# The merge of a hybrid block with its tokens stationary, and part of the weights' remainders by an adding transfer

## The chip, the core and the metric

The kernel runs on one NeuronCore of a Trainium2 chip, as one launch. The core has five engines with an instruction stream each: TensorE (PE, matrix products, with PEld for the loading of its stationary operand), VectorE (DVE), ScalarE (ACT), GpSimd (POOL) and SyncE (SP, which here issues all transfers). 16 DMA engines move data between HBM and the on-chip memory (SBUF); PE writes to a second memory, PSUM. The metric is the device time of one execution in microseconds (us); lower is better.

## What is computed

One layer of a block over 256 latent tokens of 2048 channels, with 256 context tokens beside them. All operands are fp32.

```python
u = rmsnorm(x, norm_g) * (1 + sc) + sh        # sc, sh, gt = split(silu(c) @ w_ada + b_ada)
a, g, z_c, xr, z_r, gc, gr = split(u @ w_in + b_in)          # 2048 columns each
v = depthwise_conv(a * sigmoid(g), conv_dw) + conv_dw_b      # width 31, along grid rows
y_conv = (silu(layernorm(v)) * silu(z_c)) @ w_conv_out
h = rglru(xr, forward) + rglru(xr, backward)                 # gates, short convolutions, scans
y_rnn = (h * silu(z_r)) @ w_rnn_out
y = sigmoid(gc) * y_conv + sigmoid(gr) * y_rnn               # the merge
x = rmsnorm(x + gt * (y @ w_o), final_g)
```

## The kernel before

**Products.** Each fp32 operand is split into a leading part of reduced precision (fp32r) and the remainder (`whi` and `wlo` for weights, `xh` and `xl` for activations). Each product takes three matmuls: leading by leading, leading by remainder, remainder by leading. Activations lie with the channels on the partitions, `xh[channel][tile][context or latents][token]`. The place of the context is later used for the recurrent branch's operand, then for the convolution branch's; the latents' place takes the merged result.

**Slots.** The weights are streamed in 152 blocks of 1 MB, each in two half blocks of 512 KB (`wall[s, h]`). `slot` runs one block: it asks for the loads of block s + 3 (`stage_load`), and then for each half issues that half's matmuls (`block_mms`), splits half of block s + 2 (`stage_split`), runs what was deferred and takes side work up to a budget (`run_side`). A block is 128 output channels: the 128x128 weights are stationary and 256 tokens move, 24 matmuls for each half. The slots follow `block_order`: 24 of xr and z_r, 32 of a and g, 16 of z_c, then the four matrices of the merge with 16 each, gr (72 to 87), w_rnn_out (88 to 103), gc (104 to 119) and w_conv_out (120 to 135), and 16 of w_o. The last matrix has another form already (`o_mms`): 128 tokens are stationary, 512 weight columns move, and four blocks make a chunk of 512 columns for two token tiles.

**The split.** `stage_split` has ACT make the leading part of a half block (L180), and one half later DVE subtracts it from the raw weights (L185). Raw weights have four buffers and so have the two parts. ACT thus waits until PE is through with the half block two slots back, and a load until ACT and DVE have read the raw buffer.

**Side work.** DVE's and ACT's work on the recurrence, the convolution (31 taps over 16 channel tiles, L660), the LayerNorm and the splits of its result lies in a queue of (cost, closure); `slot` takes as many as its budget allows. `BUD` (2.9 units of about a microsecond of DVE) holds from a and g through w_rnn_out, `BUD_LN` (2.6) in gc. The 64 sums for the residual gate gt (L820) come after it, two in a slot, with their own loads.

**Emptying the merge.** After a block of gr ACT takes sigmoid's tanh straight from PSUM with the channel's bias (L851). After w_rnn_out DVE multiplies (L855). gc is as gr (L863). After w_conv_out DVE multiplies and adds (L875, L876), and ACT and DVE split the sum into the latents' place (L877, helper L170 and L171), where w_o's products read it.

Of the kernel before, what the change touches and what calls it, by code (L numbers as in the profile page):

```python
# [8 lines left out]
F32 = mybir.dt.float32  # L9
# [52 lines left out]
def groups():  # L62
    """channel tiles by the order in which w_ada gives their scale and shift: (first, number)"""
    return [(k, 1) for k in range(NS1)] + [(k, 2) for k in range(NS1, KT - NE1, 2)] + [(k, 1) for k in range(KT - NE1, KT)]


def block_order():
    """the 128-channel output blocks after the first NEARLY ones: (matrix, block)"""
    seq = [("in", b) for b in XZ]
    for m in range(KT):  # L70
        seq += [("in", BA + m), ("in", BG + m)]
    seq += [("in", BZC + m) for m in range(KT)]
    seq += [("in", BGR + m) for m in range(KT)]
    seq += [("rnn", m) for m in range(KT)]
    seq += [("in", BGC + m) for m in range(KT)]
    seq += [("conv", m) for m in range(KT)]
    seq += [("o", m) for m in range(KT)]
    return seq
# [3 lines left out]
def block_kernel(ctx, tc, xcat, xtok, fgrow, par, wada, wgt, bgt, wearly, wall, wgate, out):  # L82
# [55 lines left out]
    # softplus(-lam) = max(-lam, 0) + log1p(exp(-|lam|)), log1p(e) = 2 atanh(e / (2 + e))  # L138
# [48 lines left out]

    def wsplit(raw, n=1024):
# [5 lines left out]
    def rsqrt(dst, tmp, src):  # L194
        # dst = (src + eps) ** -0.5, one Newton step on the table's value
# [7 lines left out]
    def ada_mms(acc, raw, rnd, n):  # L203
        # raw holds 8 // n channel tiles of 128 n columns of w_ada
# [7 lines left out]
    def ada_fin(row, part, k0, n):  # L212
        # sums of the four partial rows, channels to partitions
# [11 lines left out]
    def stat_mm(acc, x, i):  # L225
        # mean over channels: four column groups of the array take every fourth tile
# [10 lines left out]
    with ExitStack() as st:  # L237
# [28 lines left out]
        # with the tokens on the partitions, and back  # L266
# [27 lines left out]
        def products(m, ks, ws):  # L294
# [7 lines left out]
            # partial sums, in the end where the input's first tiles were  # L302
# [93 lines left out]
    # side work of VectorE and ScalarE between the blocks: (VectorE cost in us, closure)  # L396
# [5 lines left out]
    def defer(n, f):  # L402
        """f in n half slots"""
# [23 lines left out]
    def seg(t, d):  # L427
        # [segment][token] in the order of the scan: backward has the latents first
# [71 lines left out]
    def r_sum(h):  # L500
        # h of both directions; twice the reference's
# [30 lines left out]
    def r_tick(t):  # L532
        # stages of different half-units, interleaved so that no engine waits for itself
# [92 lines left out]
    vb = hbuf     # free by then  # L626
    tgc = vb      # the convolution's input is dead by then
# [82 lines left out]
    # LayerNorm over channels, swish, gate  # L710
# [37 lines left out]
    def ln_gates():  # L748
        # once the gate is there
# [9 lines left out]
    def ln_splits():  # L759
        # once the recurrent branch's operand is dead  # L760
# [263 lines left out]
```

## Time and profile before

| | |
|---|---|
| median of 3 runs (lowest, highest) | 1144.01 us (1144.0, 1147.85) |
| span of the profiled execution | 1142.0 us |
| the profiled execution's own time beside it | not listed apart; the runs lie from 1144.0 us |
| PE, DVE, ACT, POOL busy | 98%, 81%, 54%, 0% |
| HBM read, written | 230.25 MB, 2.10 MB |

"Busy" is time in which an engine works on an instruction; PE's matmuls overlap, so the spacing of their starts, and not their length, tells its pace. The span runs from the first to the last instruction; the measured time holds what lies around it too. A releaser, written after an arrow, is what ended an engine's wait. A stage's place in time is found by going back from the end of w_conv_out at 1043 us in steps of 16 blocks.

### The profile page before, as it was taken

To read this page: it belongs to the slowest core of one execution; us is meant where nothing else is said; L and a number is where in the kernel's file an instruction comes from. 1 tells how busy PE (TensorE), PEld (TensorE's weight loads), DVE (VectorE), ACT (ScalarE), POOL (GpSimd) and SP (SyncE) were. 2 spreads that over 40 slices of the span, in tenths; PEclk is the share of its full clock that TensorE was granted. 3 is DMA by queue.
4 is the path that set the end of the run, shared out by engine and by line. 5 is a ranking of instruction groups with operands and counts; after the bars stand their busy time and mean duration, and the time that the engine had idled before them with its cause. 6 is when DMAs were issued, how large, how long until landed. Compare 5 with 4: busy or idle time off the path is not lost.

```text
span 1142.0 us, 20720 instructions
## 1 busy us (share of the span) xinstructions
PE 1121.5 (98%) x8316; PEld 1010.7 (88%) x8316; DVE 924.9 (81%) x1528; ACT 615.1 (54%) x838; POOL 0.2 (0%) x4
## 2 busy tenths in 40 slices
PE   6999999999999999999999999999999999999996
PEld 3777778777798989999999999999999999999885
DVE  5555588789879888899998989999985977888885
ACT  3222279777888877644454444443335854444443
POOL 0000000000000000000000000000000000000000
PEclk9999999999999999999999999999999999999999
DMA  9998444233346555465555555555554569888772
GB/s 376 400 409 324 189 134 134 102 125 125 106 141 196 160 167 164 143 209 184 185 185 171 183 183 185 175 183 178 181 188 150 169 205 324 316 310 285 268 279 93
DMA packets 67635, 233.70 MB, mean 205 GB/s; under 512 B 7505, under 2 KB 11729, under 8 KB 67153
## 3 DMA queue, kind: packets, MB, share of 16 engines
q1 hardware_dynamic: 67538, 232.37, 59.5%
q8 instruction: 65, 1.06, 0.4%
q14 instruction: 32, 0.26, 0.1%
HBM read 230.25 MB, written 2.10 MB: 203 GB/s over the span
## 4 chain that ended last, share of the span: by engine, by line
PE 98%; DVE 1%; DMA 0%; ACT 0%; issue 0%; ACTq 0%; SPq 0%; DVEq 0%
PE acc L234 72%; PE o L912 8%; PE xr L234 6%; PE gate L472 5%; PE ada L209 2%; PE part L234 2%; PE ms L228 1%; DMA hbuf<-in_xcat_dram 0%; PE tp L216 0%; PE mps L228 0%; PE gps L833 0%; PE vps L228 0%; DVE sq L259 0%; DVE wlo L171 0%; PE tot L279 0%
## 5 line engine op out<-in xcount | busy, mean ns | idle before, releaser
L234 PE MATMUL acc<-xh,whi 128*128 128x256 f32 (+1 forms) x2176 | 566.8, 296 | 0.0
L234 PE MATMUL acc<-xl,whi 128*128 128x256 f32 (+1 forms) x2176 | 552.3, 289 | 0.0
L180 ACT ACTIVATE whi<-raw 128x1024 fp32r<-128x1024 f32 x304 | 321.1, 1058 | 351.0 <-PE acc L234 277.3
L234 PEld LDWEIGHTS acc<-xh,whi 128*128 128x128 f32 x2176 | 416.7, 192 | 17.8 <-issue 9.3
L234 PEld LDWEIGHTS acc<-xl,whi 128*128 128x128 f32 x2176 | 416.9, 192 | 12.5 <-issue 7.7
L185 DVE TENSOR_TENSOR wlo<-raw,whi 128x1024 fp32r<-128x1024 f32 x304 | 371.0, 1223 | 70.0 <-ACT whi L180 66.3
L234 PE MATMUL acc<-xh,wlo 128*128 128x256 f32 (+1 forms) x2176 | 319.0, 289 | 0.0
L234 PEld LDWEIGHTS acc<-xh,wlo 128*128 128x128 f32 x2176 | 288.2, 192 | 5.0
L660 DVE SCALAR_TENSOR_TENSOR cv<-hbuf,pt,cv 128x196 f32<-128x196 f32 (+14 forms) x480 | 185.9, 451 | 13.0 <-ACT cv L651 12.6
L461 DVE SCALAR_TENSOR_TENSOR xc<-xr,pt,xc 128x510 f32<-128x510 f32 (+2 forms) x96 | 71.0, 742 | 0.2
L472 PE MATMUL gate<-xc,gw 128*128 128x512 f32 x128 | 60.0, 592 | 0.0
L820 DVE SCALAR_TENSOR_TENSOR zc<-gtraw,csil,zc 128x512 f32<-128x512 f32 x64 | 47.9, 748 | 5.4 <-DMA gtraw<-in_wgt_dram 4.7
L234 PE MATMUL xr<-xh,whi 128*128 128x512 f32 x96 | 40.4, 421 | 0.4 <-ACT xh L170 0.4
L912 PE MATMUL o<-whi,xh 128*128 128x512 f32 x128 | 40.6, 399 | 0.0
L498 DVE TENSOR_TENSOR_SCAN tr<-a,ti 128x512 f32<-128x512 f32 x32 | 39.1, 1223 | 0.7
L333 ACT ACTIVATE row<-ada 128x128 f32<-128x128 f32 (+1 forms) x22 | 7.2, 326 | 60.2 <-PE ada L209 60.2
L912 PE MATMUL o<-whi,xl 128*128 128x512 f32 x128 | 39.5, 389 | 0.0
L912 PE MATMUL o<-wlo,xh 128*128 128x512 f32 x128 | 39.4, 389 | 0.0
L234 PE MATMUL xr<-xl,whi 128*128 128x512 f32 x96 | 37.7, 392 | 0.2 <-DVE xl L171 0.2
L472 PEld LDWEIGHTS gate<-xc,gw 128*128 128x128 f32 x128 | 22.8, 189 | 17.0 <-issue 13.9
L234 PE MATMUL xr<-xh,wlo 128*128 128x512 f32 x96 | 37.4, 390 | 0.0
L209 PE MATMUL ada<-adaraw,csil 128*32 128x128 f32 (+1 forms) x704 | 32.5, 324 | 1.1 <-DVE sh L218 0.9
(169 smaller groups left out, 838.1 us busy)
## 6 DMA issues: line engine op xcount, KB each, us to landing
raw<-in_wall_dram SPq DMA_DIRECT2D x304, 512.0 KB, 3.5
adaraw<-in_wada_dram SPq DMA_DIRECT2D x64, 512.0 KB, 8.5
gtraw<-in_wgt_dram SPq DMA_DIRECT2D x32, 512.0 KB, 3.9
raw<-in_wearly_dram SPq DMA_DIRECT2D x16, 512.0 KB, 9.9
gw<-in_wgate_dram SPq DMA_DIRECT2D x32, 128.0 KB, 3.2
hbuf<-in_xcat_dram SPq DMA_DIRECT2D x2, 1024.0 KB, 7.1
cv<-in_xtok_dram SPq DMA_DIRECT2D x4, 512.0 KB, 5.8
out_dram<-cv SPq DMA_DIRECT2D x6, 256.0 KB, 2.6
```

The lines of the kernel that those rows point to most:

```text
L180: A.activation(out=hi, in_=raw, func=AF.Copy)
L185: V.tensor_tensor(out=lo, in0=raw, in1=hi.bitcast(F32), op=SUB)
L209: PE.matmul(out=acc[g:g + 32, :w], lhsT=csil[:, k, :], rhs=raw[:, w * q:w * q + w], start=(k < 4), stop=(k >= KT - 4), tile_position=(0, g))
L228: PE.matmul(out=acc[32 * q:32 * q + 32, :], lhsT=ones[:, :32], rhs=x, start=(i < 4), stop=(i >= KT - 4), tile_position=(0, 32 * q))
L234: PE.matmul(out=acc, lhsT=w, rhs=x, start=(first and i == 0), stop=(last and i == n - 1))
L333: A.activation(out=row, in_=acc, func=AF.Copy)
L461: V.scalar_tensor_tensor(out=o, in0=i, scalar=w, in1=o, op0=MUL, op1=ADD)
L472: PE.matmul(out=acc, lhsT=u["gw"][:, c:c + 128], rhs=u["xc"], start=True, stop=True)
L498: V.tensor_tensor_scan(out=r(u["tr"]), data0=r(u["a"]), data1=r(u["ti"]), initial=0.0, op0=MUL, op1=ADD)
L660: V.scalar_tensor_tensor(out=o, in0=i, scalar=hdw[:, m * CW + j:m * CW + j + 1], in1=o, op0=MUL, op1=ADD)
L820: V.scalar_tensor_tensor(out=gt_chunk(c), in0=gt_raw[0][:, 512 * (k % 2):512 * (k % 2) + 512], scalar=csil[:, k, 0:1], in1=gt_chunk(c), op ...
L912: PE.matmul(out=acc, lhsT=y[:, k, 1, P * i:P * i + P], rhs=w[:, 512 * kk:512 * kk + 512], start=(k == 0 and w is hi and y is xh), stop=(k ...
```

## The change

**Form of the merge.** gr, w_rnn_out, gc and w_conv_out take the form that w_o had: the weights are packed in chunks (`chunked`), 128 tokens are stationary, 512 weight columns move (`chunk_mms`, which w_o now uses too), four slots make a chunk (`chunk_slot`, `chunks`). A half has 12 matmuls of 512 columns in place of 24 of 256. The tokens now lie on the partitions of gates and sums (`p2v`, `tgv`). The gates' bias varies along the row, so it is loaded for each chunk (`bias_load`, on SP's queue) and DVE adds it before ACT's tanh (`gate`).

**Transposes.** The merged sum has to get its channels back onto the partitions for w_o. `turn` transposes a channel tile on PE (two 128x128 transposes) and splits it into the latents' place. A chunk's four turns stand before the second, third and fourth slot of the next chunk and before the first of the one after; the last five stand behind the first halves of w_o.

**Remainders.** In slots 24 to 103, every fourth half block gets its remainder otherwise (`adding`, `wsplit_add`): ACT writes the negative leading part (a copy of the raw weights with scale -1), and a transfer issued by POOL adds the weights from HBM to it. **Budgets.** `BUD` is 3.5, the new `BUD_Y` 3.2 for gr and w_rnn_out, `BUD_LN` 3.0; the squares of the LayerNorm have 6 buffers in place of 8.

```diff
-BUD_XR, BUD_ZR, BUD_R, BUD, BUD_LN = 8.0, 2.7, 3.0, 2.9, 2.6
+BUD_XR, BUD_ZR, BUD_R, BUD, BUD_Y, BUD_LN = 8.0, 2.7, 3.0, 3.5, 3.2, 3.0
+GBB = 1
+AD0, AD1, ADN = 24, 104, 4
...
+    def wsplit_add(raw, src):
+        lo = whl_p.tile([P, 1024], F32R, tag="wlo", name="wlo")
+        A.activation(out=lo, in_=raw, func=AF.Copy, scale=-1.0)
+        nc.gpsimd.dma_start(out=lo, in_=src, accum_op=ADD)
+        return lo
...
+    def adding(s, h):
+        return AD0 <= s < AD1 and (2 * s + h) % ADN == ADN - 1
...
             raw = raws[s][h]
-            late.append(((s, h), raw, wsplit_hi(raw)))
+            hi = wsplit_hi(raw)
+            if adding(s, h):
+                parts[s, h] = hi, wsplit_add(raw, wall[s, h])
+            else:
+                late.append(((s, h), raw, hi))
...
+    def chunk_mms(acc, s, seg, kq, h, i):
+        hi, lo = parts[s, h]
+        for w, y in ((hi, xh), (hi, xl), (lo, xh)):
+            for kk in range(2):
+                k = 4 * kq + 2 * h + kk
+                PE.matmul(out=acc, lhsT=y[:, k, seg, P * i:P * i + P], rhs=w[:, 512 * kk:512 * kk + 512],
+                          start=(k == 0 and w is hi and y is xh), stop=(k == KT - 1 and w is lo))
+
+    def chunk_slot(s, seg, accs, kq, budget):
+        stage_load(s + 3)
+        for h in range(2):
+            for i in range(2):
+                chunk_mms(accs[i], s, seg, kq, h, i)
+            del parts[s, h]
+            stage_split(s + 2, h)
+            run_deferred()
+            run_side(budget / 2)
...
-    for m in range(KT):
-        acc = slot(s, lat, T, BUD)
-        A.activation(out=p2[:, m], in_=acc, func=AF.Tanh, scale=0.5, bias=hbin[:, BGR + m:BGR + m + 1])
-        s += 1
...
+    def bias_load(j, c):
+        t = tp2.tile([P, 512], F32, tag="gbias", name="gbias", bufs=GBB)
+        SP.dma_start(out=t, in_=bass.AP(brow.tensor, 2048 * j + 512 * c, [[0, P], [1, 512]]))
+        return t
+
+    def chunks(seg, budget, evac, before=None):
+        nonlocal s
+        for c in range(4):
+            accs = [psum(f"y{c}{i}") for i in range(2)]
+            for kq in range(4):
+                if before:
+                    before(c, kq)
+                chunk_slot(s, seg, accs, kq, budget)
+                s += 1
+            for i in range(2):
+                evac(c, i, accs[i])
+
+    def gate(v, c, i, acc, bias):
+        g = piece(v, c, i)
+        V.tensor_tensor(out=g, in0=acc, in1=bias, op=ADD)
+        A.activation(out=g, in_=g, func=AF.Tanh, scale=0.5)
...
+    def turn(m):
+        tps = psum("tps")[:, :T]
+        for i in range(2):
+            PE.transpose(tps[:, P * i:P * i + P], p2v[:, 2048 * i + P * m:2048 * i + P * m + P], pall("ident"))
+        split(xh[:, m, 1, :], xl[:, m, 1, :], tps)
...
+    def before_conv(c, kq):
         gt_steps(GTN)
+        m = 4 * c + kq
         if m % 2:
             o_load(m // 2)
...
+        if len(turns) > (0 if kq else 4):
+            turn(turns.popleft())
+
+    def evac_conv(c, i, acc):
+        g, t = piece(p2v, c, i), piece(tgv, c, i)
+        V.scalar_tensor_tensor(out=t, in0=t, scalar=1.0, in1=acc, op0=ADD, op1=MUL)
+        V.tensor_tensor(out=g, in0=g, in1=t, op=ADD)
+        if i:
+            turns.extend(range(4 * c, 4 * c + 4))
+
+    chunks(0, 0.0, evac_conv, before_conv)
...
                 gt_steps(GTO)
+                if turns:
+                    turn(turns.popleft())
```

On PE in w_conv_out before, the end of one block and the start of the next (`acc` is the block's sum in PSUM, `gps` a sum for gt):

```order
L234 MATMUL acc_11077<-xh,whi 128x256
L234 MATMUL acc_11077<-xl,whi 128x256
L234 MATMUL acc_11077<-xh,wlo 128x256 x8
L833 MATMUL gps<-zc,unit 128x512
L234 MATMUL acc_11150<-xh,whi 128x256
L234 MATMUL acc_11150<-xl,whi 128x256
```

The same engine and place now, one slot boundary in the second chunk (`y_9670` and `y_9671` are the sums of the two token tiles, `tps` a turn's target, `p_5045` the merged sum):

```order
L597 MATMUL y_9670<-wlo,xh 128x512 x2
L597 MATMUL y_9671<-whi,xh 128x512 x2
L597 MATMUL y_9671<-whi,xl 128x512 x2
L597 MATMUL y_9671<-wlo,xh 128x512 x2
L952 MATMUL tps<-pt,p_5045 128x128 x2
L597 MATMUL y_9670<-whi,xh 128x512 x2
L597 MATMUL y_9670<-whi,xl 128x512 x2
```

Matmuls are fewer and wider, and two transposes stand between two slots.

On DVE in w_conv_out before, one slot (`zc` takes the sums for gt, `hbuf` is the gate, `p_5033` the merged sum):

```order
L820 SCALAR_TENSOR_TENSOR zc<-gtraw,csil,zc 128x512 x2
L875 SCALAR_TENSOR_TENSOR hbuf<-hbuf,acc_10730 128x256
L876 TENSOR_TENSOR p_5033<-p_5033,hbuf 128x256
L171 TENSOR_TENSOR xl<-p_5033,xh 128x256
L185 TENSOR_TENSOR wlo<-raw,whi 128x1024 x2
```

And now, the end of the second chunk there and the first slot of the third:

```order
L188 TENSOR_TENSOR wlo<-raw,whi 128x1024 x2
L968 SCALAR_TENSOR_TENSOR hbuf<-hbuf,y_9670 128x512
L969 TENSOR_TENSOR p_5045<-p_5045,hbuf 128x512
L968 SCALAR_TENSOR_TENSOR hbuf<-hbuf,y_9671 128x512
L969 TENSOR_TENSOR p_5045<-p_5045,hbuf 128x512
L858 SCALAR_TENSOR_TENSOR zc<-gtraw,csil,zc 128x512 x2
L174 TENSOR_TENSOR xl<-tps,xh 128x256
L188 TENSOR_TENSOR wlo<-raw,whi 128x1024 x2
```

The multiplying and adding moved from each slot to the end of a chunk, four wide steps in a row; the split's subtraction now follows a transpose.

On ACT at the end of z_c before (`whi` is a leading part, `cv` the convolution's sum):

```order
L180 ACTIVATE whi<-raw 128x1024 x2
L790 ACTIVATE zc<-acc_7099,pt 128x256
L180 ACTIVATE whi<-raw 128x1024 x2
L651 ACTIVATE cv<-hbuf,pt 128x256 x2
L851 ACTIVATE p_5033<-acc_7169,hbin 128x256
L180 ACTIVATE whi<-raw 128x1024 x2
L851 ACTIVATE p_5033<-acc_7240,hbin 128x256
```

And now, on the same engine through the first chunk of gr:

```order
L183 ACTIVATE whi<-raw 128x1024 x2
L194 ACTIVATE wlo<-raw 128x1024
L828 ACTIVATE zc<-acc_7174,pt 128x256
L183 ACTIVATE whi<-raw 128x1024 x4
L194 ACTIVATE wlo<-raw 128x1024
L689 ACTIVATE cv<-hbuf,pt 128x256 x2
L183 ACTIVATE whi<-raw 128x1024 x4
L194 ACTIVATE wlo<-raw 128x1024
L915 ACTIVATE p_5045<-p_5045 128x512 x2
```

After four leading parts stands a negative copy into a remainder's buffer, and the tanh of a gate comes twice per chunk instead of once per slot.

## Rows read from the trace of the kernel before

**Rows 1.** The page, parts 1 and 4: busy time, and the chain's engines.

```profile
span 1142.0 us, 20720 instructions
...
PE 1121.5 (98%) x8316; PEld 1010.7 (88%) x8316; DVE 924.9 (81%) x1528; ACT 615.1 (54%) x838; POOL 0.2 (0%) x4
...
PE 98%; DVE 1%; DMA 0%; ACT 0%; issue 0%; ACTq 0%; SPq 0%; DVEq 0%
```

**Rows 2.** Windows: stages z_c, gr, w_rnn_out, gc and w_conv_out, with the header.

```profile
core 0: us, PE busy (x) PEld busy (x) DVE busy (x) ACT busy (x) POOL busy (x), PEclk, DMA share, GB/s
575.00:667.00 92.00, 92.00 (x765) 90.91 (x764) 83.42 (x157) 42.18 (x52) 0.00 (x0) 1.00 0.57 183
667.00:759.60 92.60, 92.60 (x770) 91.51 (x769) 82.03 (x155) 42.09 (x53) 0.00 (x0) 1.00 0.56 180
759.60:851.60 92.00, 92.00 (x764) 90.91 (x764) 86.31 (x167) 34.63 (x36) 0.00 (x0) 1.00 0.56 180
851.60:949.90 98.30, 98.30 (x817) 94.92 (x816) 70.43 (x116) 61.02 (x99) 0.00 (x0) 1.00 0.59 190
949.90:1043.00 93.10, 93.10 (x772) 92.62 (x771) 80.78 (x112) 41.39 (x50) 0.00 (x0) 1.00 0.89 315
```

**Rows 3.** Chain in order of time: start us, us, engine, out, line.

```profile
859.00 0.43 PE tot L717 x2
...
996.91 46.07 PE acc L234 x384
...
1077.37 43.56 PE o L912 x192
```

**Rows 4.** Groups by line and shape: count, busy us, mean ns, idle before.

```profile
L185 DVE TENSOR_TENSOR wlo<-raw,whi 128x1024 fp32r<-128x1024 f32 x304 | 371.0, 1223 | 70.0 <-ACT whi L180 66.3 <-ACT a L478 0.6
...
L180 ACT ACTIVATE whi<-raw 128x1024 fp32r<-128x1024 f32 x304 | 321.1, 1058 | 351.0 <-PE acc L234 277.3 <-DMA raw<-in_wall_dram 22.1 <-PE o L912 20.9
...
L820 DVE SCALAR_TENSOR_TENSOR zc<-gtraw,csil,zc 128x512 f32<-128x512 f32 x64 | 47.9, 748 | 5.4 <-DMA gtraw<-in_wgt_dram 4.7
...
L171 DVE TENSOR_TENSOR xl<-p,xh 128x256 fp32r<-128x256 f32 x16 | 6.8, 425 | 8.2 <-ACT xh L170 8.2
...
L897 DVE TENSOR_TENSOR cv<-cv,hbuf 128x512 f32<-128x512 f32 x8 | 5.5, 693 | 0.3
...
L896 DVE SCALAR_TENSOR_TENSOR hbuf<-o,zc 128x512 f32<-128x512 f32 x8 | 5.5, 687 | 4.8 <-PE o L912 4.8
```

**Rows 5.** Timeline of PE over one half block: start us, us, instruction.

```profile
700.36 0.28 PE L234 MATMUL acc<-xh,whi 128*128 128x256 f32 x1
...
702.28 1.12 PE L234 MATMUL acc<-xh,wlo 128*128 128x256 f32 x8
703.24 0.28 PE L234 MATMUL acc<-xh,whi 128*128 128x256 f32 x1
```

**Rows 6.** Timeline of ACT in the same half block.

```profile
702.48 1.06 ACT L180 ACTIVATE whi<-raw 128x1024 fp32r<-128x1024 f32 x1 [1.44 <-PE acc L234]
```

**Rows 7.** DMA issues: count, KB each, median us from issue to landing.

```profile
raw<-in_wall_dram SPq DMA_DIRECT2D x304, 512.0 KB, 3.5
...
raw<-in_wearly_dram SPq DMA_DIRECT2D x16, 512.0 KB, 9.9
```

**Rows 8.** Groups by line, DVE alone, 460 to 860 us.

```profile
L660 DVE SCALAR_TENSOR_TENSOR cv<-hbuf,pt,cv 128x196 f32<-128x196 f32 (+14 forms) x480 | 185.9, 451 | 13.0 <-ACT cv L651 12.6
L185 DVE TENSOR_TENSOR wlo<-raw,whi 128x1024 fp32r<-128x1024 f32 x136 | 166.5, 1225 | 20.3 <-ACT whi L180 18.3
...
L718 DVE COPY mean<-tot 128x256 f32<-128x256 f32 x1 | 0.4, 424 | 2.0 <-PE tot L717 2.0
L712 DVE COPY rstd<-mps 128x256 f32<-128x256 f32 x1 | 0.4, 418 | 0.0
```

**Rows 9.** The page, part 2: DMA share and GB/s in 40 slices.

```profile
DMA  9998444233346555465555555555554569888772
GB/s 376 400 409 324 189 134 134 102 125 125 106 141 196 160 167 164 143 209 184 185 185 171 183 183 185 175 183 178 181 188 150 169 205 324 316 310 285 268 279 93
```

More of the change, by code (lines that the diff above doesn't have):

```diff
@@ L29 @@
 TA, TB, TC, TD = 1, 2, 1, 1
+AD0, AD1, ADN = 24, 104, 4
 SG = 4
+CHUNKED = ("gr", "rnn", "gc", "conv", "o")
 BA, BG, BZC, BXR, BZR, BGC, BGR = 0, 16, 32, 48, 64, 80, 96
@@ L72, in block_order, with block_kernel @@
     seq += [("in", BZC + m) for m in range(KT)]
[L73 to L77, printed above, removed]
+    for a in CHUNKED:
+        seq += [(a, m) for m in range(KT)]
     return seq
 @with_exitstack
-def block_kernel(ctx, tc, xcat, xtok, fgrow, par, wada, wgt, bgt, wearly, wall, wgate, out):
+def block_kernel(ctx, tc, xcat, xtok, fgrow, brow, par, wada, wgt, bgt, wearly, wall, wgate, out):
     nc = tc.nc
@@ L847, in o_load @@
             SP.dma_start(out=fgb[:, c:c + 1024], in_=bass.AP(fgrow.tensor, c, [[0, P], [1, 1024]]))
-    for m in range(KT):
-        acc = slot(s, lat, T, BUD)
-        A.activation(out=p2[:, m], in_=acc, func=AF.Tanh, scale=0.5, bias=hbin[:, BGR + m:BGR + m + 1])
-        s += 1
-    for m in range(KT):
-        acc = slot(s, ctxp, T, BUD)
-        V.scalar_tensor_tensor(out=p2[:, m], in0=p2[:, m], scalar=1.0, in1=acc, op0=ADD, op1=MUL)
-        s += 1
+    p2v = p2.rearrange("p k t -> p (k t)")
@@ new lines, in block_kernel, with piece @@
+    tgv = vb.rearrange("p k t -> p (k t)")
+    def piece(v, c, i):
+        return v[:, 2048 * i + 512 * c:2048 * i + 512 * c + 512]
+    def bias_load(j, c):
[13 more added lines that the diff above has]
+                evac(c, i, accs[i])
@@ new lines, in gate, with before_gr, evac_rnn @@
+    def gate(v, c, i, acc, bias):
+        g = piece(v, c, i)
+        V.tensor_tensor(out=g, in0=acc, in1=bias, op=ADD)
+        A.activation(out=g, in_=g, func=AF.Tanh, scale=0.5)
+    gbias = {}
+    def before_gr(c, kq):
+        if kq == 1:
+            gbias[c] = bias_load(0, c)
+    chunks(1, BUD_Y, lambda c, i, acc: gate(p2v, c, i, acc, gbias[c]), before_gr)
+    def evac_rnn(c, i, acc):
+        g = piece(p2v, c, i)
+        V.scalar_tensor_tensor(out=g, in0=g, scalar=1.0, in1=acc, op0=ADD, op1=MUL)
@@ L857, in block_kernel, with before_gc, evac_gc @@
+    chunks(0, BUD_Y, evac_rnn)
     ln["rnn"] = True
     ln_splits()
-    for m in range(KT):
-        acc = slot(s, lat, T, BUD_LN)
-        while m not in conv_done:
+    def before_gc(c, kq):
+        if kq == 1:
+            gbias[c] = bias_load(1, c)
+        gt_steps(GTG)
+    def evac_gc(c, i, acc):
+        while any(m not in conv_done for m in (8 * i + 2 * c, 8 * i + 2 * c + 1)):
             run_side(0.5)
-        A.activation(out=tgc[:, m], in_=acc, func=AF.Tanh, scale=0.5, bias=hbin[:, BGC + m:BGC + m + 1])
-        gt_steps(GTG)
-        s += 1
+        gate(tgv, c, i, acc, gbias[c])
@@ L866, in block_kernel @@
+    chunks(1, BUD_LN, evac_gc, before_gc)
     while side or any(queue):
@@ L868, in block_kernel @@
         run_deferred()
-    for m in range(KT):
-        acc = slot(s, ctxp, T, 0.0)
+    def turn(m):
[3 more added lines that the diff above has]
+        split(xh[:, m, 1, :], xl[:, m, 1, :], tps)
+    turns = deque()
+    def before_conv(c, kq):
         gt_steps(GTN)
+        m = 4 * c + kq
         if m % 2:
             o_load(m // 2)
-        V.scalar_tensor_tensor(out=tgc[:, m], in0=tgc[:, m], scalar=1.0, in1=acc, op0=ADD, op1=MUL)
-        V.tensor_tensor(out=p2[:, m], in0=p2[:, m], in1=tgc[:, m], op=ADD)
-        split(xh[:, m, 1, :], xl[:, m, 1, :], p2[:, m])
-        s += 1
+        if len(turns) > (0 if kq else 4):
[7 more added lines that the diff above has]
+    chunks(0, 0.0, evac_conv, before_conv)
     ssq = tp2.tile([P, 2, 4], F32, tag="ssq", name="ssq", bufs=1)
@@ L904, in last @@
     def last(i):
-        return p2[:, 2 * i:2 * i + 2].rearrange("p a t -> p (a t)")
-    def o_mms(acc, s, kq, h, i):
-        hi, lo = parts[s, h]
-        for w, y in ((hi, xh), (hi, xl), (lo, xh)):
-            for kk in range(2):
-                k = 4 * kq + 2 * h + kk
-                PE.matmul(out=acc, lhsT=y[:, k, 1, P * i:P * i + P], rhs=w[:, 512 * kk:512 * kk + 512],
-                          start=(k == 0 and w is hi and y is xh), stop=(k == KT - 1 and w is lo))
+        return piece(p2v, 0, i)
     def finish(i):
@@ L985, in tiles, with chunked @@
         return w.reshape(KT, P, -1, P).transpose(2, 1, 0, 3)
-    mats = {"in": tiles(i["w_in"][0]), "conv": tiles(i["w_conv_out"][0]), "rnn": tiles(i["w_rnn_out"][0])}
-    wo = i["w_o"][0].reshape(4, 2, 2, P, 4, 512).transpose(4, 0, 1, 3, 2, 5).reshape(KT, 2, P, 1024)
-    wall = np.stack([wo[m] if a == "o" else mats[a][m].reshape(P, 2, 1024).transpose(1, 0, 2)
+    def chunked(w):
+        return w.reshape(4, 2, 2, P, 4, 512).transpose(4, 0, 1, 3, 2, 5).reshape(KT, 2, P, 1024)
+    win = i["w_in"][0]
+    mats = {"in": tiles(win), "gr": chunked(win[:, P * BGR:]), "gc": chunked(win[:, P * BGC:P * BGR]),
+            "rnn": chunked(i["w_rnn_out"][0]), "conv": chunked(i["w_conv_out"][0]), "o": chunked(i["w_o"][0])}
+    wall = np.stack([mats[a][m] if a in CHUNKED else mats[a][m].reshape(P, 2, 1024).transpose(1, 0, 2)
                      for a, m in block_order()])
```

9 lines of the change are left out of this document (5 added, 4 removed).

## The prediction

> **What bounds the kernel now.** I read the shares of busy time and the chain of waits first, to see which engine the end hangs on. TensorE (PE) is busy 98% of the span, and the chain that ended last runs 98% through its matmuls [rows 1]. Then the busy time by stage: from 575 to 1043 us, where the gated merge and its side work lie, PE is busy in every microsecond of each stretch, while VectorE (DVE) is busy 72% to 94% and ScalarE (ACT) 38% to 62% [rows 2]. So in this stretch only PE's own issue time shortens the run, until another engine or a transfer falls so far behind that PE has to wait for it. Last, the chain in order of time gives PE's pace: 384 matmuls of 256 columns in 46.07 us are 120.0 ns each, and 192 of 512 columns, the form of the output projection, in 43.56 us are 226.9 ns each [rows 3]. Twice the columns cost 106.9 ns more, so 13.1 ns of each matmul don't depend on its width.
>
> **What the merge's new form takes off PE.** The four matrices have 64 slots. Before, a slot has 48 matmuls, 48 x 0.1200 = 5.76 us; now it has 24 of 512 columns, in the operand form of the output projection, 24 x 0.2269 = 5.445 us. That is 0.315 us a slot and 64 x 0.315 = 20.2 us in all. Both paces are measured in this trace behind the same kind of weight loading (one per matmul), and nothing else on PE changes there, so I take the whole 20.2.
>
> **What the transposes put back.** There are 32 of 128 columns, two in each of 16 turns; the trace has no transpose. From above: an ordinary fp32 product of 256 columns takes 0.43 us in two passes (the row of tot in [rows 3]), so 128 columns are 0.215, and 32 x 0.215 = 6.9 us. From below: one pass at the pace of the 256-column matmul, 106.9 / 2 + 13.1 = 66.5 ns, 32 x 0.0665 = 2.1 us. A gain is excluded, since they are additional instructions on the busy engine. I take 4.0, between the two. A transpose also waits: for the four DVE steps that empty a chunk, 2 x (0.687 + 0.693) = 2.8 us [rows 4]. The first turn of a chunk stands behind a whole slot of 5.445 us, that of the fourth chunk behind two halves of the output projection, so 2.7 us are left for what DVE has queued before. Behind a waiting transpose all of PE stands; I price this wait at nothing, and at 16 x 0.5 = 8 us if DVE is late.
>
> **DVE and ACT.** Of 160 half blocks in slots 24 to 103, 40 no longer have a DVE remainder of 1.223 us, 49 us less on DVE, and get a second ACT pass of 1.058 us, 42 us more on ACT [rows 4]. Neither comes off the end, because PE is the bound. The added budget for side work spends the freed DVE time: in the z_c stage DVE is busy 83.42 us in 16 slots, of which 32 x 1.223 = 39.1 are remainders, so 44.3 us stand for 16 x 2.9 = 46.4 units of budget, 0.95 us a unit. In the gated stages four slots now hold 6 x 1.223 + 4 x 3.2 x 0.95 + 2 x 0.69 = 20.9 us of DVE work in 21.8 us of PE, 96% (94% before in the recurrent product [rows 2]). In the last stage of the merge it is 8 x 1.223 + 8 x 0.748 + 2.8 + 4 x 0.425 = 20.3 of 21.8, 93% against 87%. The two gates' bias moves to DVE, 16 additions of 0.69 = 11 us; their tanh on ACT goes from 32 narrow to 16 wide ones. The side work ends sooner in slots: 16 x (0.6 + 0.3 + 0.3) units are more than six slots' worth, so the sums for the residual gate start earlier and are not late at the end. All this costs nothing while DVE stays under PE; that cover is thin.
>
> **SP's queue.** Eight loads of a bias (256 KB, each waiting until the chunk before has given its buffer back) are issued between the weights' loads, and what is queued behind them are the weights three slots ahead. The buffer comes free some 3 us into the chunk's first slot and the load stands in the second, so I cost it at nothing; one slot of delay would still leave the weights two slots.
>
> **The adding transfers.** This is the large unknown: PE needs the remainder by a deadline. In a block of 256 columns a half starts at 700.36, its remainder products at 702.28, and ACT starts the next leading part for that buffer at 702.48 [rows 5, 6]. ACT is done with it at 703.54 and with the negative copy at 704.60; four halves later, at 711.88 + 1.92 = 713.80, PE reads the remainder. So 9.2 us are left for issue on POOL, transfer and landing. In a chunk the half lasts 2.72 us, the buffer is free after 10 of 12 matmuls, ACT ends at 2.27 + 0.2 + 2 x 1.06 = 4.6, and PE reads at 10.89 + 0.91 = 11.8: 7.2 us are left. A plain transfer of the same 512 KB lands 3.5 us after its issue at this load, and 9.9 us in the start phase where the queues are full [rows 7]. An adding one reads its target as well; as an estimate it takes one to three times 3.5, that is 3.5 to 10.5 us. I take 6, nearer to the row at the same load, and so no wait. The Trainium skill, "DMA: Bandwidth & Descriptors", section "Anatomy of one DMA — SWDGE (gpsimd) path", gives 2.0 us plus the bytes at 436 GB/s for a plain transfer issued by GpSimd; that would be an estimate of 3.2 us, and no row here shows one.
>
> **Sum.** The profiled execution has a span of 1142.0 us [rows 1] and the median is 1144.01, so 2.0 us lie around the span. 1144.0 - 20.2 + 4.0 = 1127.8, say 1128 us.
>
> **Rivals.**
> 1. *The remainder lands late (slower).* POOL's transfers get through only after the deadline, and PE stands still once per adding half block. Each microsecond over 7.2 costs 16 us (16 such halves in chunks), each over 9.2 another 24. The gain of 16.2 us is gone at 8.2 us. At the 9.9 us of the slow row it is 16 x 2.7 + 24 x 0.7 = 60 us, and 1188 us. For it: the adding read, DMA engines already 55% busy [rows 2], POOL has done no transfer so far. Against it: about half the engines' time is free there, and the load is a third larger at most. The Trainium skill, "SBUF — State Buffer", section "SBUF: two separate sides" (the box on the "DVE blocks DMA" trap), warns of just such transfers: GpSimd cannot write descriptors while VectorE runs an operation in a two-port mode, a copy for instance. In the stretch of the adding halves DVE's time is nearly all two-source operations, with two copies of 0.4 us [rows 8], so by this page they would not be held up; no run here shows it yet.
> 2. *DVE or the transfers become the bound.* With 96% in 32 slots a few microseconds of waits per chunk suffice for DVE to run behind, and half of these stages' gain would go: 32 x 0.315 / 2 = 5 us. In the last stage of the merge DMA moves 315 GB/s at a share of 0.89; at the new pace the same bytes need 315 x 5.76 / 5.445 = 333 GB/s, a share of 0.94, where the start phase shows up to 409 GB/s [rows 2, 9]. If loads hold PE there, the stage keeps its old length, 16 x 0.315 = 5 us. Each gives 1133, both with late transposes 1146.
> 3. *The pace doesn't improve.* If a wide matmul cost per column what a narrow one costs, 240 ns, the gain is nil and the transposes remain: 1148 us. The rows of the output projection speak against it. The Trainium skill, "TensorE: Matmul & The Clock Gate", section "Back-to-back issue gap", has a fixed part of only about 2.5 ns per matmul; by it 24 fewer matmuls in 64 slots bring an estimate of 3.8 us and the time stays at 1144. The measured part is 13.1 ns, and the measurement decides.
>
> **How the numbers follow.** Forecast (no wait that PE feels): 0.64, with its own range of 1125 to 1132. Rival 1: 0.17, nearly all of it slower than before. Rival 2: 0.15, of that 0.12 still clearly faster. Rival 3: 0.04. About 0.5%, 5.7 us, is what a measurement of this kernel can tell from no change. Faster than 1138.3: 0.64 + 0.12 = 0.76, and a little of rival 1, 0.77. Within: 0.03 + 0.04 = 0.07, with rival 1's part 0.08. Slower than 1149.7: 0.15. The range starts below the cheapest transposes (1144.0 - 20.2 + 2.1 = 1125.9), at 1124, and goes to 1146, where rival 2 in full ends and rival 1 has an average lateness of about half a microsecond.
>
> **What would show it.** Right: 24 matmuls in about 5.45 us in all four stages, PE idle under 3 us between 390 and 1120 us, turns of 0.13 to 0.43 us, adding transfers landing under 7 us after issue. Wrong: PE waiting for POOL's transfer once in two slots (rival 1); PE waiting for DVE's remainder or for a chunk's emptying, or ACT's leading parts released by late loads (rival 2); a pace near 240 ns (rival 3).

## The result: slower, and the profile after

The changed kernel takes 1156.28 us (median of 4 runs, 1151.54 to 1156.87), the kernel before 1145.32 on the same chip (1144.0 to 1147.85). The ratio is 1.0083 with a 95% interval of [1.0059, 1.0107]: slower by 0.8%, where 1128 us were forecast, and outside the range. The profile is of the fastest of the four runs, with a span of 1149.8 us; what the other three have more, some 5 us, no trace shows. Nearly all of the 24 us between the forecast for the span (1142.0 - 16.2 = 1125.8) and the profile lie in two stages.

The page of the changed kernel, parts 1, 3 and 4, which answers to [rows 1]:

```profile
span 1149.8 us, 17801 instructions
...
PE 1112.7 (97%) x6812; PEld 933.4 (81%) x6812; DVE 884.9 (77%) x1480; ACT 647.8 (56%) x862; POOL 34.9 (3%) x44
...
q0 software_dynamic: 5760, 20.97, 10.3%
...
PE 82%; DMA 11%; ACT 2%; DVE 2%; issue 2%; SPq 0%; ACTq 0%; POOLq 0%; DVEq 0%
```

PE's share of busy time fell by one point only, and a reader who stops there sees nothing. The chain of waits shows it: DMA, which had 0%, now has 11%. The windows by stage, z_c, gr, w_rnn_out, gc and w_conv_out, with the columns of [rows 2], each from the first matmul of its matrix to that of the next:

```profile
573.20:667.60 94.40, 94.40 (x783) 92.77 (x782) 85.54 (x181) 50.66 (x62) 6.92 (x8) 1.00 0.80 225
...
667.60:766.00 98.40, 90.95 (x394) 71.59 (x393) 81.98 (x168) 46.24 (x52) 6.92 (x8) 1.00 0.82 226
766.00:871.60 105.60, 96.87 (x430) 74.21 (x429) 77.79 (x150) 60.21 (x80) 6.92 (x8) 0.97 0.72 198
871.60:959.50 87.90, 87.90 (x387) 72.43 (x386) 68.35 (x86) 43.02 (x56) 0.00 (x0) 1.00 0.82 282
959.50:1051.00 91.50, 91.50 (x411) 74.75 (x410) 73.45 (x90) 39.00 (x48) 0.00 (x0) 1.00 0.89 311
```

The borders of [rows 2], found by going back from the end, miss the first matmuls by up to 2 us. By the first matmuls, gr, w_rnn_out, gc and w_conv_out before are:

```profile
665.10:758.70 93.60, 93.60 (x778) 92.51 (x777) 83.58 (x157) 41.83 (x53) 0.00 (x0) 1.00 0.56 181
758.70:853.00 94.30, 94.30 (x783) 92.67 (x781) 86.85 (x169) 36.58 (x38) 0.00 (x0) 1.00 0.56 180
853.00:949.80 96.80, 96.80 (x806) 93.97 (x805) 69.86 (x115) 59.88 (x98) 0.00 (x0) 1.00 0.59 191
949.80:1043.30 93.50, 93.50 (x775) 92.78 (x773) 81.16 (x113) 41.66 (x50) 0.00 (x0) 1.00 0.89 314
```

The z_c stage still has blocks of 256 columns, and 8 adding transfers (the count under POOL); PE has no gap there. In gr and w_rnn_out, in chunks of 512 columns with 8 such transfers each, PE is idle for 7.5 and 8.7 us. In gc and w_conv_out, in chunks but without such transfers, PE is busy throughout and the stages are shorter than before by 8.9 and 2.0 us. Together the four stages of the merge take 383.4 us, against 378.2 before and about 361 by the forecast (378.2 - 20.2, and 2.7 for the eleven of the sixteen turns that lie in w_conv_out).

What PE waits for, from the view of waits, and the same for its weight loading. The columns are the us waited in total, how many times, and the longest. The weight loads (PEld) are the better measure, because the ends of PE's matmuls are modelled:

```profile
PE y L597 <- DMA wlo<-in_wall_dram: 16.0, 11, 6.0
PE acc L244 <- DMA wlo<-in_wall_dram: 0.6, 1, 0.6
...
PEld y L597 <- DMA wlo<-in_wall_dram: 22.0, 14, 6.4
...
PEld acc L244 <- DMA wlo<-in_wall_dram: 0.8, 1, 0.8
```

y is a chunk's sum, acc that of a 256-column block. Sixteen chunk halves have an adding transfer and cost 22.0 us; 24 block halves cost 0.8. One period of the loss, from the chain in order of time in gr (start us, us, what):

```profile
704.28 1.05 ACT wlo L194
705.34 0.28 issue
705.62 8.08 DMA wlo<-in_wall_dram
713.70 0.04 issue
713.74 1.67 PE y L597 x6
...
716.45 1.05 ACT wlo L194
717.50 0.28 issue
717.79 8.68 DMA wlo<-in_wall_dram
```

It is a closed ring: the negative copy on ACT, 0.28 us to POOL's start, 8.1 us of transfer, the half's last matmuls, and the next copy into the buffer that they gave back. The timeline of POOL gives its period:

```profile
669.18 0.86 POOL L195 DMA_DIRECT2D wlo<-in_wall_dram  x1 [11.40 <-ACT wlo L194]
...
730.56 0.86 POOL L195 DMA_DIRECT2D wlo<-in_wall_dram  x1 [11.91 <-ACT wlo L194]
```

There is one such transfer per two slots, and six issues in 669.18 to 730.56 are five periods of 12.28 us. Two slots of the new form are 2 x 5.445 = 10.89. So 1.39 us are lost per transfer in this stretch. That 16 x 1.39 = 22.2 us is so close to the 22.0 of the waits is partly chance: one of those waits, the 6.4 us, has another cause, a copy that started late in w_rnn_out (see below), and the others share 15.6. The DMA issues, answering to [rows 7] (us from issue to landing at the end of the row), show the size that was wrong:

```profile
raw<-in_wall_dram SPq DMA_DIRECT2D x304, 512.0 KB, 4.4
...
wlo<-in_wall_dram POOLq DMA_DIRECT2D x40, 512.0 KB, 8.0
```

### The profile page after: what moved, and what is told of

Read it like the earlier page. It is cut to its first block, busy times and chain, and to the rows that moved or that the text cites. A ratio compares the mean times of both kernels' runs of the same rounds, so it can differ in the third digit from the quotient of the medians.

```text
span 1149.8 us, 17801 instructions
## 1 busy us (share of the span) xinstructions
PE 1112.7 (97%) x6812; PEld 933.4 (81%) x6812; DVE 884.9 (77%) x1480; ACT 647.8 (56%) x862; POOL 34.9 (3%) x44
## 3 DMA queue, kind: packets, MB, share of 16 engines
q0 software_dynamic: 5760, 20.97, 10.3%
## 4 chain that ended last, share of the span: by engine, by line
PE 82%; DMA 11%; ACT 2%; DVE 2%; issue 2%; SPq 0%; ACTq 0%; POOLq 0%; DVEq 0%
PE acc L244 38%; PE y L597 20%; DMA wlo<-in_wall_dram 9%; PE o L597 8%; PE xr L244 6%; PE gate L490 5%; PE ada L219 2%; PE part L244 2%; DMA adaraw<-in_wada_dram 1%; ACT wlo L194 1%; DMA xhi<-in_xcat_dram 1%; DVE cv L698 1%; ACT whi L183 0%; DVE wlo L188 0%; PE tp L226 0%
## 5 line engine op out<-in xcount | busy, mean ns | idle before, releaser
L244 PE MATMUL acc<-xh,whi 128*128 128x256 f32 (+1 forms) x1152 | 313.9, 306 | 0.0
L244 PE MATMUL acc<-xl,whi 128*128 128x256 f32 (+1 forms) x1152 | 301.1, 295 | 0.0
L244 PEld LDWEIGHTS acc<-xh,whi 128*128 128x128 f32 x1152 | 220.3, 191 | 13.8 <-issue 6.5
L244 PEld LDWEIGHTS acc<-xl,whi 128*128 128x128 f32 x1152 | 220.4, 191 | 12.2 <-issue 7.4
L597 PE MATMUL y<-wlo,xh 128*128 128x512 f32 x512 | 160.5, 395 | 16.2 <-DMA wlo<-in_wall_dram 16.0
L244 PE MATMUL acc<-xh,wlo 128*128 128x256 f32 (+1 forms) x1152 | 175.5, 295 | 0.6 <-DMA wlo<-in_wall_dram 0.6
L597 PE MATMUL y<-whi,xh 128*128 128x512 f32 x512 | 161.1, 396 | 0.0
L244 PEld LDWEIGHTS acc<-xh,wlo 128*128 128x128 f32 x1152 | 156.1, 191 | 5.9 <-DMA wlo<-in_wall_dram 0.8
L597 PE MATMUL y<-whi,xl 128*128 128x512 f32 x512 | 158.5, 391 | 0.0
L597 PEld LDWEIGHTS y<-whi,xl 128*128 128x128 f32 x512 | 96.4, 188 | 20.6
```

Source lines behind the costliest of these rows:

```text
L244: PE.matmul(out=acc, lhsT=w, rhs=x, start=(first and i == 0), stop=(last and i == n - 1))
L597: PE.matmul(out=acc, lhsT=y[:, k, seg, P * i:P * i + P], rhs=w[:, 512 * kk:512 * kk + 512], start=(k == 0 and w is hi and y is xh), stop=( ...
```

## The experiments

Four theories were set against each other. A: the chunk halves read the adding remainder before it has landed, since the ring above gives it 7.2 us and it needs 8.3 (0.28 from the copy to POOL and 8.0 to landing). B: an adding transfer costs the same wherever it stands. C: DVE, the emptying of chunks or another part of the new merge holds PE, and the transfers only happen to be named. D, which came up later: the sums for the residual gate crowd the last stages. Edits are against the changed kernel unless said otherwise.

**Adding transfers only in the blocks** (the 24 block halves; in gr and w_rnn_out DVE makes the remainders again, and the budget for side work goes back with them):

```
-BUD_XR, BUD_ZR, BUD_R, BUD, BUD_Y, BUD_LN = 8.0, 2.7, 3.0, 3.5, 3.2, 3.0
+BUD_XR, BUD_ZR, BUD_R, BUD, BUD_Y, BUD_LN = 8.0, 2.7, 3.0, 3.5, 2.6, 3.0
-AD0, AD1, ADN = 24, 104, 4
+AD0, AD1, ADN = 24, 72, 4
```

> The changed kernel with adding transfers only in the 24 half blocks of slots 24 to 71 (256-column form); the 16 in the two chunked stages get their remainder from VectorE again, and the side-work budget there falls from 3.2 to 2.6 so that VectorE stays at about 97%. Theory A (the 16 chunked halves read the remainder before it has landed, about 1.3 us each): 1127 to 1134 us. Theory B (each adding transfer costs about the same wherever it stands, by its traffic or its extra ScalarE pass): 24 of 40 remain, 1138 to 1145 us. Theory C (VectorE or the emptying of chunks holds TensorE in the gated stages, transfers or not): 1147 us or more.

Measured: 1135.04 us (1134.37 to 1135.64), ratio to before 0.9911 [0.9896, 0.9926]. This is 21 us under the changed kernel and clearly faster than before. The 24 transfers still land after 7.9 us, and PE waits for one of them once:

```profile
PE tps L952 <- DVE p L969: 1.8, 3, 0.9
PE y L597 <- DVE wlo L188: 1.3, 1, 1.3
...
PE acc L244 <- DMA wlo<-in_wall_dram: 0.5, 1, 0.5
```

So the loss belongs to the chunk halves, and what is left are small waits for DVE.

**Adding transfers only in the chunks**:

```
-... = 8.0, 2.7, 3.0, 3.5, 3.2, 3.0
+... = 8.0, 2.7, 3.0, 2.9, 3.2, 3.0
-AD0, AD1, ADN = 24, 104, 4
+AD0, AD1, ADN = 72, 104, 4
```

> The changed kernel with adding transfers only in the 16 half blocks of slots 72 to 103 (chunked form), and the budget in the 256-column stages back at 2.9. Theory A (the remainder is read before it lands, in the chunked form only): the loss stays, 1148 to 1158 us. Theory B (each transfer costs the same anywhere): 16 of 40 remain, 1135 to 1142 us. Theory C (VectorE): as without any transfer or somewhat better, 1132 to 1140 us.

Measured: 1149.72 us (1144.87 to 1156.9), ratio 1.0032 [1.0009, 1.0055]. The gain is still gone, and the waits are those of the changed kernel at 70% of the size (the weight loads wait 16.9 us in place of 22.0, and none of these waits is over 2.6):

```profile
PE y L597 <- DMA wlo<-in_wall_dram: 11.3, 11, 2.2
```

**The kernel before, plus adding transfers** in the same 40 halves, all of them of 256 columns there (against the kernel before):

```
+AD0, AD1, ADN = 24, 104, 4
...
-            late.append(((s, h), raw, wsplit_hi(raw)))
+            hi = wsplit_hi(raw)
+            if adding(s, h):
+                parts[s, h] = hi, wsplit_add(raw, wall[s, h])
+            else:
+                late.append(((s, h), raw, hi))
```

> The kernel before with nothing but the adding transfers, 40 half blocks in slots 24 to 103, all of them in the 256-column form, budget 2.9 as before. Theory A: 9.2 us are allowed after the negative copy and 8.3 needed, so nearly no wait: 1144 to 1149 us. Theory B: 40 times about half a microsecond more than before, 1160 us or more. Theory C: as before, 1143 to 1146 us, since VectorE only gets lighter.

Measured: 1147.87 us (1144.9 to 1149.86), ratio 1.0013 [1.0, 1.0026]. Forty transfers with the same landing time cost PE one wait of half a microsecond:

```profile
wlo<-in_wall_dram POOLq DMA_DIRECT2D x40, 512.0 KB, 8.0
```

```profile
PE acc L241 <- DMA wlo<-in_wall_dram: 0.5, 1, 0.5
```

With 9.2 us allowed a landing of 8.0 is hidden. This rules out B. It also shows that freed DVE time alone is worth nothing where PE is the bound.

**No adding transfers at all**, the new merge alone:

```
-... = 8.0, 2.7, 3.0, 3.5, 3.2, 3.0
+... = 8.0, 2.7, 3.0, 2.9, 2.6, 3.0
-AD0, AD1, ADN = 24, 104, 4
+AD0, AD1, ADN = 0, 0, 4
```

> The changed kernel without any adding transfer, all remainders from VectorE, budgets 2.9 in the 256-column stages (as before) and 2.6 in the two gated chunked stages. Theory A: the merge's new form alone, 1126 to 1132 us. Theory B: the same. Theory C: 1145 us or more, since VectorE carries 49 us more than in the changed kernel.

Measured: 1139.15 us (1137.85 to 1142.47), ratio 0.9953 [0.9938, 0.9968]. The merge alone is faster than before, but some 10 us are missing against what theory A expected: a miss. Some 7.5 of them are in the last stage, w_conv_out, which takes 99.0 us (in the changed kernel 91.5), and now it is DVE that PE waits for:

```profile
938.80:1037.80 99.00, 93.38 (x410) 75.27 (x409) 74.50 (x92) 37.61 (x45) 0.00 (x0) 0.98 0.84 294
```

```profile
DVE zc L858 <- DMA zc<-in_bgt_dram: 6.8, 1, 6.8
...
PE y L597 <- DVE wlo L188: 4.4, 2, 3.9
PE tps L952 <- DVE p L969: 2.0, 4, 1.0
```

(tps are the transposes; the first row is a wait of DVE, in the first step of the sums for the residual gate.) With the smaller budgets the side work runs later, and the 64 sums for the residual gate fall into the last stage. That is theory D, tried by the next two.

**No sums for the residual gate**: the kernel without adding transfers, and of it the 64 steps of those sums and their 32 loads left out, so that the gate is its bias alone. **Narrow sums**: the loads kept, each step on 8 of 512 columns, so that the gate is summed on these columns only.

```
-        for n in range(GTB):
-            gt_load(n)
...
-        V.scalar_tensor_tensor(out=gt_chunk(c), in0=gt_raw[0][:, 512 * (k % 2):512 * (k % 2) + 512],
-                               scalar=csil[:, k, 0:1], in1=gt_chunk(c), op0=MUL, op1=ADD)
```

```
-        V.scalar_tensor_tensor(out=gt_chunk(c), in0=gt_raw[0][:, 512 * (k % 2):512 * (k % 2) + 512],
-                               scalar=csil[:, k, 0:1], in1=gt_chunk(c), op0=MUL, op1=ADD)
+        o = 512 * (k % 2)
+        V.scalar_tensor_tensor(out=gt_chunk(c)[:, :8], in0=gt_raw[0][:, o:o + 8],
+                               scalar=csil[:, k, 0:1], in1=gt_chunk(c)[:, :8], op0=MUL, op1=ADD)
```

> The version without any adding transfer (1139 us), with the 64 steps of the residual gate's sums and their 32 loads left out, so that the gate is its bias alone. Theory D (its 10 us over the forecast come from the residual gate's work, which starts late there and crowds the last two stages): 1126 to 1132 us. Theory C (VectorE or the emptying of chunks holds TensorE in the gated stages themselves): 1136 us or more.

> The version without any adding transfer, with the residual gate's loads kept but its 64 steps on 8 columns in place of 512 (the rest of the gate is its bias). If theory D holds by VectorE's time (64 x 0.75 us): 1126 to 1132 us, as without the steps. If it holds by the 16 MB of loads in the last stages: 1135 to 1140 us, as with the full steps. Theory C: 1136 us or more.

Measured: 1131.85 us without the sums (1130.45 to 1132.06), ratio 0.9882 [0.9868, 0.9897], and 1135.41 with narrow ones (1133.56 to 1136.32), ratio 0.9914 [0.9899, 0.9930]. Against 1139.15, 3.7 of the 7.3 us are DVE's time for the wide steps and the other 3.6 come with the loads and what is left of the steps. The second part is mainly one wait and not crowding: in both versions that have the loads DVE stands 6.8 and 7.0 us in the first step, for loads that SP issued only just before, and the weights' remainders behind that step on DVE make PE wait 3.9 and 2.9 us. Without the sums the last stage has about the forecast's length, 93.5 - 5.0 + 2.7 = 91.2:

```profile
938.60:1029.30 90.70, 90.70 (x409) 74.36 (x408) 52.89 (x60) 38.77 (x47) 0.00 (x0) 1.00 0.71 232
```

**Blocks only, at a larger budget** in the gated stages (against blocks only):

```
-... = 8.0, 2.7, 3.0, 3.5, 2.6, 3.0
+... = 8.0, 2.7, 3.0, 3.5, 2.9, 3.0
```

> As the version with adding transfers in slots 24 to 71 only, but with a side-work budget of 2.9 instead of 2.6 in the gated chunked stages, so that VectorE's work for the LayerNorm and the residual gate comes earlier while it has 8 x 1.22 + 4 x 2.9 x 0.95 + 1.4 = 22.2 us of work in 21.8 there. If lateness of the later side work cost that version its last 4 us: 1129 to 1134 us. If VectorE is the limit in the gated stages (theory C): 1136 to 1142 us.

Measured: 1136.78 us (1136.54 to 1137.35), ratio 0.9920 [0.9905, 0.9934]. The interval overlaps that of blocks only: nothing is gained. The time lies in theory C's range, but that does not show C: in its profile PE waits 3.1 us for DVE's remainders, and this wait too begins with DVE standing, 5.4 us, for the first loads of the residual gate's sums; and the start phase ran some 2 us longer, so the two don't separate cleanly.

**Remainder products last.** Each half first does the leading products of both its token tiles and then the remainder products of both, so that PE reads the remainder four matmuls, 0.91 us, later:

```
-            for i in range(2):
-                chunk_mms(accs[i], s, seg, kq, h, i)
+            for part in (0, 1):
+                for i in range(2):
+                    chunk_mms(accs[i], s, seg, kq, h, i, part)
```

> The changed kernel, all 40 adding transfers kept; in each half of a chunk both token tiles' leading products come first and the remainder products last, so that the remainder is read 8 instead of 4 matmuls into the half (0.9 us later) and the leading part's buffer comes free 0.45 us earlier. Theory A: the deadline moves by about 1.35 us, so nearly all of the waits of about 1.3 us go: 1130 to 1140 us. Theory B and theory C: the order of these matmuls is of no account, 1149 to 1157 us.

Measured: 1144.46 us (1139.69 to 1151.46), ratio 0.9991 [0.9971, 1.0011]. About 12 of the 22 us came back, less than expected:

```profile
PE y L597 <- DMA wlo<-in_wall_dram: 8.0, 4, 4.5
```

It fits the ring: the read comes 0.91 us later, and the leading part's buffer, whose copy stands before the negative one on ACT, is free 0.45 us earlier, so about 8.5 us are allowed where 8.3 are needed. The median just fits, and single late landings (10.1 us at most) still hold PE. The longest of the four waits, 4.5 us, is again the late copy in w_rnn_out.

**The same transfers, not adding.** POOL moves the same bytes at the same times but overwrites; the remainder of these 40 halves is then the weight itself:

```
-        nc.gpsimd.dma_start(out=lo, in_=src, accum_op=ADD)
+        nc.gpsimd.dma_start(out=lo, in_=src)
```

> The changed kernel with POOL's 40 transfers plain instead of adding (they overwrite the negative copy, so the remainder of these half blocks is the weight itself and the product is wrong by that part). If the adding is what makes a transfer land 8.0 us after its issue, the plain one lands in 4 to 5 us, as those of SP, and the time is 1127 to 1133 us. If it is POOL's own path, it lands in 7 to 8 us and the time stays at 1147 to 1157 us.

Measured: 1138.39 us (1135.46 to 1141.27), ratio 0.9933 [0.9908, 0.9958], between the two expectations. Queue, landing and wait:

```profile
q0 software_dynamic: 5760, 20.97, 5.3%
...
wlo<-in_wall_dram POOLq DMA_DIRECT2D x40, 512.0 KB, 6.1
```

```profile
PE y L597 <- DMA wlo<-in_wall_dram: 5.2, 1, 5.2
```

The landing falls from 8.0 to 6.1 us, under the 7.2 allowed, and PE's waits fall to one, which is the late copy in w_rnn_out once more: a faster transfer doesn't remove that one. So the addition itself costs 1.9 us per transfer (0.34 of it in POOL's own instruction) and decides whether the deadline is met; the rest, 6.1 against the 4.2 of SP's transfers in this run, goes with the other queue and was not taken apart.

**The remainder started one half earlier**, into two buffers of its own (which the residual gate's loads share later), with the bytes, the order of PE and the budgets unchanged:

```
-        lo = whl_p.tile([P, 1024], F32R, tag="wlo", name="wlo")
+        lo = wla_p.tile([P, 1024], F32R, tag="wla", name="wla")
...
-                parts[s, h] = hi, wsplit_add(raw, wall[s, h])
+                parts[s, h] = hi, early.pop((s, h))
...
+            if h == 0 and adding(s, 1):
+                early[s, 1] = wsplit_add(raws[s][1], wall[s, 1])
```

> The changed kernel, all 40 adding transfers kept, but the negative copy and the transfer are issued one half block earlier (2.7 us in a chunk), into two buffers of their own, which the loads for the residual gate use later. Theory A: the deadline becomes about 9.9 us against 8.3 to 9.5 needed, the waits go: 1127 to 1134 us. Theory B: traffic and passes are the same, 1148 to 1157 us. Theory C: the same as B.

Measured: 1133.16 us (1131.34 to 1137.42), ratio 0.9900 [0.9873, 0.9926], the lowest median of the versions that leave nothing out, and faster than both kernels. Its interval overlaps that of blocks only (0.9911), so it isn't shown that adding transfers in the chunks, started early, are worth more than none there. The landing is still 7.9 us, but with 7.2 + 2.72 = 9.9 us allowed it is hidden. Waits, chain, and the windows of gr and w_rnn_out:

```profile
PE y L599 <- DMA wla<-in_wall_dram: 1.6, 1, 1.6
...
PE y L599 <- DVE wlo L188: 0.8, 1, 0.8
```

```profile
PE 96%; issue 2%; DMA 1%; DVE 1%; ACT 0%; ACTq 0%; SPq 0%; POOLq 0%; DVEq 0%
```

```profile
666.30:755.00 88.70, 88.70 (x395) 72.27 (x394) 82.00 (x168) 47.01 (x52) 6.74 (x8) 1.00 0.86 249
755.00:851.20 96.20, 93.77 (x430) 73.34 (x429) 74.90 (x148) 58.60 (x78) 6.24 (x8) 1.00 0.74 210
```

The gr stage goes from 98.4 to 88.7 us, with the same work and the same number of transfers. This shows A for the chunks: the distance between issue and use was changed, and with it the buffers (DVE's remainders now have the four `wlo` buffers to themselves); remainder products last, above, moved the distance without more buffers.

**Earlier and remainder last together**, the two edits above in one kernel:

> The version with the adding transfers issued half a block earlier, and in addition the remainder products last in each half of a chunk: 0.9 us more to the deadline. If single late landings (10.4 us at most) still cost that version its last 3 to 5 us: 1128 to 1132 us. If not: 1131 to 1136 us, no different.

Measured: 1136.0 us (1130.58 to 1136.92), ratio 0.9905 [0.9876, 0.9935], no different from the version before. Once the transfer has its time, more distance is worth nothing that these runs can tell.

## Why the prediction was wrong, step by step

The step that failed is the one on the adding transfers: "I take 6, nearer to the row at the same load, and so no wait". The allowance of 7.2 us in a chunk was right (the plain, the remainder-last and the early versions behave by it), and so was the allowance of 9.2 us in a block. The landing was mis-sized: 8.0 us plus 0.28 us from the copy's end to the start on POOL, 8.3 in all. The range I gave for it, 3.5 to 10.5, held 8.0; the choice within it was wrong, and since the deadline lay inside the range, the choice decided the sign. I took a plain SP transfer's 3.5 us and some for the extra read. Measured, POOL's transfer takes 6.1 us before any addition, and the addition 1.9 more.

Rival 1 is what happened, with the end that it named: PE waiting once in two slots, in the chunks and not in the blocks. Its own sum is close. At 8.3 us it gives 16 x 1.1 = 17.6 us, against 22.0 measured, of which 15.6 belong to the ring (16.9 in the version with adding transfers in the chunks only). The other 6.4 are a late copy in w_rnn_out, which no term of the prediction had: it let the copy start as soon as its buffer was free, which would be at about 842 here, but the LayerNorm's steps on DVE held up ACT (the copy at 847.41, landing at 856.37). The larger budgets had brought these steps forward into w_rnn_out; before, they lay in gc, as the rows of tot in [rows 3] show. The versions with remainder products last and with plain transfers have this wait too, with 4.5 and 5.2 us; in the early one 1.6 us are left of it. PE stood for 6.0 us:

```profile
856.41 1.22 PE L597 MATMUL y<-wlo,xh 128*128 128x512 f32 x2 [6.01 <-DMA wlo<-in_wall_dram]
857.43 1.05 PE L597 MATMUL y<-whi,xh 128*128 128x512 f32 x2
858.28 1.05 PE L597 MATMUL y<-whi,xl 128*128 128x512 f32 x2
```

While it stood, the granted clock fell to the lower of its two levels, 1.2 GHz, and the matmuls behind the wait start 0.43 us apart in place of 0.23, which costs about another 1.8 us over eight of them:

```profile
853.20:860.00 6.80, 3.59 (x9) 2.83 (x10) 6.00 (x13) 3.92 (x6) 0.00 (x0) 0.50 0.87 246
```

Its chance of 0.17 was too low for a cost that no row of before showed and whose deadline lay inside its bounds.

The other terms held:

- The pace of the new form. 344 matmuls in 78.27 us are 227.5 ns each, against 226.9 taken from [rows 3], so rival 3 is out. The Trainium skill's fixed part of about 2.5 ns per matmul ("TensorE: Matmul & The Clock Gate", "Back-to-back issue gap") isn't what these matmuls show; the section gives it for a single matmul's gap, and says itself that in a stream with a weight load for each matmul both set the spacing. These matmuls, with one weight load each, keep about the 13.1 ns that the two paces of before gave.
- The transposes. In the last stage a slot with a turn is 999.12 to 1004.81, 5.69 us, or 0.24 us over 5.445. That is 16 x 0.24 = 3.9 us, where 4.0 were taken. Chain of the changed kernel:

```profile
869.63 78.27 PE y L597 x344
947.90 0.86 PE gps L871 x2
...
999.12 0.22 PE tps L952 x2
999.34 5.47 PE y L597 x24
1004.81 0.22 PE tps L952 x2
```

- The last two stages, which have both terms and no adding transfers, take 87.9 + 91.5 = 179.4 us. Before they took 96.8 + 93.5 = 190.3, of which 4.6 us (96.8 less 16 x 5.76) are the LayerNorm's products, which lay in gc before [rows 3] and now lie in w_rnn_out (its 430 PE records against 394 in gr). The forecast takes off 32 x 0.315 and puts back eleven turns of 0.25, 7.3 in all, which gives 178.4; a sum for gt on PE (`gps`), 0.9 us, has moved into gc besides.
- DVE's cover. It was called thin at 96%. In the early version gr has DVE busy 82.00 of 88.70 us, 92%, and PE waits for it once, 0.8 us. Rival 2 did not decide here, but the run without adding transfers shows how near it was: 7.3 us hang on the sums for the residual gate, on DVE's time for them and on their loads, for which DVE stands with the remainders behind it. So the time that the adding transfers free on DVE is of use (blocks only has a ratio of 0.9911, no adding transfers 0.9953), and only the way it was freed in the chunks was too slow.
- SP's queue. No wait of PE leads back to the eight bias loads. ACT waits more for weights than before (56.4 us against 22.1 in [rows 4]), as its row shows, but PE does not wait for ACT's leading parts in the chunks:

```profile
L183 ACT ACTIVATE whi<-raw 128x1024 fp32r<-128x1024 f32 x220 | 232.9, 1060 | 279.5 <-PE y L597 105.8 <-PE acc L244 90.8 <-DMA raw<-in_wall_dram 56.4
```

The sum closes for the profiled run: the forecast for its span was 1125.8 us, and 22.0 + 0.8 of waits for the adding remainder make it 1148.6, with the 1.8 of the slower clock 1150.4, against 1149.8 measured. The early version, at 1129.6, is 3.8 us above the forecast; 2.4 of these are the waits shown, and the rest was not traced.

The Trainium skill's figures for a GpSimd-issued transfer ("DMA: Bandwidth & Descriptors", "Anatomy of one DMA — SWDGE (gpsimd) path") gave an estimate of 3.2 us for 512 KB in the prediction. The plain POOL transfer landed after 6.1 us here, beside other transfers, at a DMA share of 0.66 to 0.76 in that run's gated stages; the measurement decides. Whether the trap that the Trainium skill describes in "SBUF — State Buffer", "SBUF: two separate sides", adds to it was not tried: no run changed DVE's modes in that stretch.

## What to carry to other kernels

When work goes from a busy engine to a transfer, first write down the time from the release of the buffer to its next read, and then ask how long that transfer takes in its own kind and on its own queue. If the deadline lies inside the bounds, the forecast has two signs, and the cheapest edit that makes the answer not matter (an earlier start into a buffer of its own) belongs in the change from the start. A faster consumer also shortens every deadline that is counted in its steps: the same transfer was hidden at 2.88 us per half and late at 2.72, because the wide chunk gives its buffers back later and reads them sooner. Of the 2.0 us between the two allowances, 9.2 and 7.2, the four shorter halves take 0.6, the earlier read within the half 1.0, and the later return of the buffer the rest.

## What the runs showed of the hardware

- An adding transfer of 512 KB, issued by POOL, landed after 8.0 us (median of 40); the same without the addition after 6.1 us, and SP's of the same size after 4.4, all beside other traffic.
- It also takes twice the DMA engines' time: 10.3% of 1149.8 us over 40 transfers is 3.0 us of all 16 engines each, against 5.3% of 1135.3, 1.5 us, for the plain ones. POOL's own instruction takes 0.87 and 0.53 us.
- A transpose of a 128x128 fp32 tile has one record on PE: a pair adds 0.24 us to the matmuls' time, where an ordinary fp32 product of 256 columns has two records and takes 0.43 us [rows 3].
